# The two exponentials of the SSD chunk decays, moved behind the last logarithm of the GLA gates on ScalarE

## The chip, the core and the metric

The kernel runs on one core of a Trainium2 chip. The metric is the time of one execution on the device, in microseconds (us); lower is better. TensorE is called PE in the profile, VectorE DVE, ScalarE ACT, GpSimd POOL, and SyncE, which issues nearly all DMAs, SP. PEld is TensorE's load of the stationary operand.

## The reference

One layer of a hybrid encoder is applied to a prompt of 256 tokens and a sample of 512 tokens, each of width 1024. The input is normed and projected by one matrix (`w_in`), and three mixers share the result: a gated linear attention (GLA, 4 heads), a differential attention (4 heads) and a state space mixer (SSD, 8 heads). Their outputs go through `w_out`, and an MLP of width 4096 follows. GLA and SSD both run forwards and backwards over the tokens. Two pieces of it matter here:

```
# GLA: the gates
logg_f = jax.nn.log_sigmoid((r_f @ wg_f + bg_f)) / GLA_GATE_NORM

# SSD: steps, and the decay of the state over one chunk
dt_f = jax.nn.softplus(sdt[..., :SSD_HEADS] + dtb_f)
la = dt * a_neg
acum = jnp.cumsum(la, axis=1)
state = state * jnp.exp(acum[:, -1]) + ...
```

The last line's factor, the exponential of the sum of `la` over a whole chunk, is what the edit moves. The kernel computes it for six chunks of 128 tokens, two directions and eight heads.

## The kernel before, in words

All 768 tokens are worked on together as NT = 6 tiles of 128 tokens. Products with weights are split into high and low fp32r parts: a weight unit comes from DRAM in two halves (`wr`, two buffers), ScalarE casts the high part (`wh`, L134), VectorE subtracts to get the low part (`wl`, L135), and TensorE makes three matmuls per product (L98 to L100). `wh` and `wl` have two buffers each. `fm_unit` makes products with features on partitions (PSUM tiles `fm`, from the pool of three accumulators), `tm_unit` those with tokens on partitions (`tm`, the same pool). All other PSUM tiles (`tms`, `tmb`, `gate`, `kTp`, `U`, `att`) share the five buffers called `mx`.

The kernel is one straight program. A planner simulates all engines and fixes from it, before the kernel runs, the order of the instructions in each engine's queue; program order decides between instructions that are ready. On the chip each queue runs in order, with semaphores between the queues. `tc.high_priority()` lets instructions go ahead in that order. `tc.issue_after(ins)` keeps the instructions written inside it behind `ins` in the queue of that engine; it adds no semaphore.

Around the change the program is, in this order:

- `gla_v(0)`, then small loads and `glr_unit`, which gives the inputs of the GLA gates (`rst`) and of the SSD steps (`zdt`, 16 partitions).
- `ssd_dt()` (L503 to L564), called at L1034. Absolute value, exponential, logarithm and a correction give the softplus (L507 to L517). VectorE makes the running sums in each tile (`inc`, L522, called `dpre` in the profile) and the exclusive sums (`exc`, `dexc`, L523). SyncE writes both to DRAM (`scr`, L533 and L534), and the last column of `inc` to `scp` (L535). L538 reads `scp` back, broadcast to all partitions, as `ptb`. L543 takes two exponentials of it, one per half of the partitions, into `decs`. Then TensorE transposes the stacked rows (`tms`, L550; `tmb`, L555), ScalarE copies them out of PSUM (L552, L556), takes four exponentials of them (`ew`, L558 to L561), and VectorE multiplies two of those (L562, L563).
- `gla_gates(0)` and `gla_gates(1)` (L263 to L294), called at L1035. Each makes, for two directions, a gate product in two matmuls of 512 and 256 columns (L274), their absolute values and rectified values on ScalarE (L276, L277), one exponential (L278) and one logarithm (L279); VectorE adds and makes the running sums (L282 to L292). The list `log_ins` collects the four logarithms; the kernel's `tanh` (L196) uses its last entry with `issue_after`, since the tanh needs another function table in ScalarE.
- `gla_qk(0)`, `gla_core(pre[0], ...)` and so on (L1070 to L1077). The core's exponentials (L347 to L359) give `kst`, TensorE transposes it (`kTp`, L371), makes the states' products (`U`, L381), and then seven levels of differences (L428), exponentials (L432, L437), products (`eq`, L433, on VectorE; `ek`, L438, on GpSimd) and small matmuls (`att`, L412).

The planner interleaves these: matmuls of `gla_qk` fill TensorE while the gates run. The reader of `decs` is L660 in `ssd_states`, long after both GLA cores.

Of the kernel before, what the change touches and what calls it, by code (L numbers as in the profile page):

```python
# [13 lines left out]
AF = mybir.ActivationFunctionType  # L14
# [28 lines left out]
def hybrid_kernel(ctx, tc, io):  # L43
    nc = tc.nc
    mm, act, dve, pool = nc.tensor.matmul, nc.scalar, nc.vector, nc.gpsimd
# [10 lines left out]
    def nm(s):  # L56
        uid[0] += 1
        return f"{s}_{uid[0]}"
# [28 lines left out]
    def mx(name):  # L87
        return psm.tile([P, 512], F32, tag="mx", name=nm(name))
# [4 lines left out]
    def bc(ap, shape):  # L93
        return ap.to_broadcast(shape)
# [99 lines left out]
    log_ins = []  # L194
# [57 lines left out]
    def v128(t):  # L252
        return t.rearrange("p (c w) -> p c w", w=P)

    def prefix(dst, lg):

        dve.tensor_tensor_scan(dst, resetm[:dst.shape[0]], lg, 0.0, ALU.mult, ALU.add)
# [5 lines left out]
    def gla_gates(hp):  # L263


        c0 = hp * P
        pre = []
        for d, r in ((0, R_BF), (1, R_BB)):
            bias, nbias = col(r + hp), nbf[:, 2 * d + hp:2 * d + hp + 1]
            rngs = ((0, 512), (512, 256))  # L270
            zs = [mx("gate"), mx("gate")]
            t1, g = t3("gt1"), t3("gt2")
            for z, (o, n) in zip(zs, rngs):
                mm(z[:, :n], lhsT=wg[d][0:96, c0:c0 + P], rhs=rst[0:96, o:o + n], start=True, stop=True)  # L274
            for z, (o, n) in zip(zs, rngs):
                act.activation(t1[:, o:o + n], z[:, :n], AF.Abs, bias=bias)  # L276
                act.activation(g[:, o:o + n], z[:, :n], AF.Relu, bias=nbias, scale=-1.0)  # L277
            act.activation(t1, t1, AF.Exp, scale=-1.0)  # L278
            log_ins.append(act.activation(t1, t1, AF.Ln, bias=1.0).ins)  # L279
            pf = s3("pre")  # L280
            if d == 0:
                dve.tensor_tensor(g, g, t1, ALU.add)  # L282
                prefix(pf, g)
                pre.append(pf)
            else:
                tot = const.tile([P, NT, 1], F32, name=nm("tot"))
                dve.scalar_tensor_tensor(tot, v128(g)[:, :, 127:128], -1.0, v128(t1)[:, :, 127:128], op0=ALU.mult, op1=ALU.subtract)
                dve.scalar_tensor_tensor(v128(pf)[:, :, 1:128], v128(g)[:, :, 0:127], -1.0, v128(t1)[:, :, 0:127],
                                         op0=ALU.mult, op1=ALU.subtract)
                pool.memset(v128(pf)[:, :, 0:1], 0.0)  # L290
                prefix(pf, pf)
                dve.tensor_tensor(tot, tot, v128(pf)[:, :, 127:128], ALU.add)  # L292
                pre += [pf, tot]
        return pre  # L294
# [208 lines left out]
    def ssd_dt():  # L503

        ps_ = slice(96, 112)
        z, t1, u, l = zdt[ps_], t3("dz")[ps_], t3("dt2")[ps_], t3("dl")[ps_]
        act.activation(t1, z, AF.Abs)  # L507
        act.activation(t1, t1, AF.Exp, scale=-1.0)
        act.activation(l, t1, AF.Ln, bias=1.0)
        dve.tensor_scalar(u, t1, 1.0, -1.0, op0=ALU.add, op1=ALU.add)  # L510
        dve.tensor_tensor(t1, t1, u, ALU.subtract)
        act.activation(u, l, AF.Exp, scale=-1.0)
        dve.tensor_tensor(t1, t1, u, ALU.mult)
        dve.tensor_tensor(l, l, t1, ALU.add)
        stk = t3("stk")
        pool.memset(stk, 0.0)
        dve.scalar_tensor_tensor(stk[0:16], z, 0.0, l, op0=ALU.max, op1=ALU.add)  # L517
        dtl = t3("dtl")[ps_]

        dve.tensor_scalar(dtl, stk[0:16], sdtc[0:16, 3:4], -128.0, op0=ALU.mult, op1=ALU.max)  # L520
        inc, exc = t3("dpre")[ps_], t3("dexc")[ps_]
        dve.tensor_tensor_scan(inc, resetm[ps_], dtl, 0.0, ALU.mult, ALU.add)  # L522
        dve.tensor_tensor(exc, inc, dtl, ALU.subtract)  # L523
        act.copy(stk[32:48], inc)
        act.copy(stk[64:80], exc)
        tot = bc(v128(inc)[:, :, 127:128], [16, NT, P])
        dve.tensor_tensor(v128(stk[96:112]), tot, v128(inc), ALU.subtract)
        stb = t3("stb")
        dve.tensor_tensor(v128(stb[0:16]), tot, v128(exc), ALU.subtract)

        scr = dram.tile([16, T], F32, name="scr")
        scp = dram.tile([16, NT], F32, name="scp")
        nc.sync.dma_start(out=scr[0:8, :], in_=inc[0:8])  # L533
        nc.sync.dma_start(out=scr[8:16, :], in_=exc[8:16])  # L534
        nc.sync.dma_start(out=scp, in_=v128(inc)[:, :, 127])  # L535

        ptb = const.tile([P, 2, 8, NT], F32, name="ptb")
        nc.sync.dma_start(out=ptb.rearrange("p d h c -> p (d h c)"),  # L538
                            in_=bc(scp.rearrange("h c -> (h c)")[None, :], [P, 16 * NT]))
        decs = const.tile([P, NT, 2, 4], F32, name="decs")  # L540
        for g in range(2):
            gs = slice(64 * g, 64 * g + 64)
            act.activation(decs[gs], ptb[gs, :, 4 * g:4 * g + 4, :].rearrange("p d h c -> p c d h"), AF.Exp)  # L543

        tms = const.tile([P, NT, 40], F32, name="tms")
        tmb = const.tile([P, NT, 16], F32, name="tmb")
        for (a, b) in ((0, 4), (4, 6)):
            ps = mx("tms")
            for c in range(a, b):
                nc.tensor.transpose(ps[:, (c - a) * P:(c - a) * P + 112], stk[0:112, c * P:(c + 1) * P], ident[0:112, 0:112])  # L550
            for o, r, n in ((0, 0, 16), (16, 32, 8), (24, 72, 8), (32, 96, 8)):
                act.copy(tms[:, a:b, o:o + n], v128(ps)[:, :b - a, r:r + n])  # L552
        ps = mx("tmb")
        for c in range(NT):
            nc.tensor.transpose(ps[:, 16 * c:16 * c + 16], stb[0:16, c * P:(c + 1) * P], ident[0:16, 0:16])  # L555
        act.copy(tmb, ps[:, :96].rearrange("p (c r) -> p c r", c=NT))  # L556
        ew = const.tile([P, NT, 2, 2, 8], F32, name="ew")
        act.activation(ew[:, :, 0, 0, :], tms[:, :, 16:24], AF.Exp)  # L558
        act.activation(ew[:, :, 0, 1, :], tmb[:, :, 8:16], AF.Exp)
        act.activation(ew[:, :, 1, 0, :], tms[:, :, 32:40], AF.Exp)  # L560
        act.activation(ew[:, :, 1, 1, :], tms[:, :, 24:32], AF.Exp)  # L561
        dve.tensor_tensor(ew[:, :, 1, 0, :], ew[:, :, 1, 0, :], tms[:, :, 0:8], ALU.mult)  # L562
        dve.tensor_tensor(ew[:, :, 1, 1, :], ew[:, :, 1, 1, :], tms[:, :, 8:16], ALU.mult)  # L563
        return scr, decs, tms, ew  # L564

    def ssd_conv(us, xt, bcm):
        def conv(j):
# [417 lines left out]
    for i, nme in enumerate(("gla_wg_f", "gla_wg_b")):  # L985
# [4 lines left out]
        g = wgt[:, 256 * i:256 * i + 256]  # L990
# [30 lines left out]
    def col(r):  # L1021
        return cols[:, r:r + 1]
# [8 lines left out]
    qg8 = const.tile([P, 1], F32, name="qg8")  # L1031
    dve.tensor_scalar(qg8, col(R_QN), 0.125, None, op0=ALU.mult)

    dt = ssd_dt()  # L1034
    pre = [gla_gates(hp) for hp in range(2)]  # L1035

    masks = t2("masks").bitcast(U8)[:, :len(LOCAL) * 32].rearrange("p (l i) -> p l i", i=32)
    mraw = t2("mraw", n=len(LOCAL) * 32).rearrange("p (l i) -> p l i", i=32)
# [11 lines left out]
    for i in range(2):  # L1050
        g = qk16[:, i, None, :]
# [172 lines left out]
```

## Time and profile before

| | us |
|---|---|
| median of 3 runs | 1169.85 |
| lowest and highest | 1168.61, 1171.22 |
| the profiled execution | 1169.03 |
| its span, first to last instruction | 1167.2 |
| PE, DVE, ACT, POOL busy | 1110.8, 737.8, 563.9, 157.0 |

TensorE is busy in 95% of the span, at a mean granted clock of 0.976 of full speed. Matmuls are pipelined and their ends are modelled, so busy is not the same as at the peak. [...] The shares over the whole span tell little of a change in one place; the rows further down are read from the stretch around the edited lines, 60 to 110 us from the span's start, and from the first GLA core behind it.

### The profile page before, as it was taken

How to read it: one execution, taken by the hardware profiler on the slowest of the kernel's cores; microseconds unless marked ns; L12 is line 12 of the kernel's file. 1: busy time of each engine (PE TensorE's matmuls, PEld its weight loads, DVE VectorE, ACT ScalarE, POOL GpSimd, SP SyncE). 2: the span in 40 equal slices, each digit the busy share in tenths (PEclk: the TensorE clock that was granted, in tenths of full speed). 3: DMA queues.
4: the chain of work that ended last, by engine and by line, in shares of the span. 5: the costliest groups of instructions: out<-in, count | busy, mean ns of one | idle time of the engine just before them, and what ended most of it. 6: DMA issues, size and time to landing. Idle time of an engine off the chain costs nothing.

```text
span 1167.2 us, 19741 instructions
## 1 busy us (share of the span) xinstructions
PE 1110.8 (95%) x7868; PEld 978.6 (84%) x7868; DVE 737.8 (63%) x1298; ACT 563.9 (48%) x1119; POOL 157.0 (13%) x208
## 2 busy tenths in 40 slices
PE   7989797999998999899989999999999999999998
PEld 6989697999998986788877897788887787787786
DVE  6559859563697668887677786846544534434443
ACT  7476666554377237756666573425231332322321
POOL 1002425310401360110100012200000000000000
PEclk9989798899999999899999999999999999999999
DMA  6312021171534355445543549522323323233231
GB/s 196 85 40 74 4 64 38 41 240 39 162 96 127 111 160 167 126 144 177 195 144 120 187 145 305 200 92 73 108 72 108 101 80 108 77 104 99 82 109 72
DMA packets 118642, 136.41 MB, mean 117 GB/s; under 512 B 8936, under 2 KB 86790, under 8 KB 118550
## 3 DMA queue, kind: packets, MB, share of 16 engines
q1 hardware_dynamic: 118517, 135.14, 36.6%
q8 instruction: 62, 1.02, 0.3%
q14 instruction: 31, 0.25, 0.1%
q10 hardware_dynamic: 32, 0.01, 0.0%
HBM read 121.44 MB, written 13.68 MB: 116 GB/s over the span
## 4 chain that ended last, share of the span: by engine, by line
PE 61%; DVE 16%; DMA 11%; ACT 6%; issue 3%; POOL 2%; SPq 0%; DVEq 0%; ACTq 0%; POOLq 0%
PE tp L98 7%; DMA wr<-in_w_mlp 7%; PE tp L99 7%; PE tp L100 7%; PE fm L98 6%; PE fm L100 6%; PE fm L99 6%; PE tm L100 5%; PE tm L99 5%; PE tm L98 5%; DVE wl L135 4%; ACT wh L134 2%; DMA er<-scr 1%; DVE d L428 1%; DVE eq L433 1%
## 5 line engine op out<-in xcount | busy, mean ns | idle before, releaser
L134 ACT CAST wh<-wr 128x1024 fp32r<-128x1024 f32 x186 | 189.2, 1048 | 236.5 <-PE tp L100 129.2
L135 DVE TENSOR_TENSOR wl<-wr,wh 128x1024 fp32r<-128x1024 f32 x186 | 224.2, 1229 | 93.4 <-ACT wh L134 92.8
L100 PE MATMUL tm<-wh,hTl 128*128 128x256 f32 x576 | 168.7, 293 | 0.0
L98 PE MATMUL tm<-wh,hTh 128*128 128x256 f32 x576 | 166.8, 290 | 0.5 <-ACT xp L576 0.5
L99 PE MATMUL tm<-wl,hTh 128*128 128x256 f32 x576 | 166.8, 290 | 0.0
L901 DVE TENSOR_TENSOR xres<-tp,xres 128x512 f32<-128x512 f32 x116 | 77.8, 687 | 100.5 <-PE tp L100 100.3
L99 PEld LDWEIGHTS tm<-wl,hTh 128*128 128x128 f32 x576 | 112.4, 195 | 1.5 <-issue 1.0
L98 PEld LDWEIGHTS tm<-wh,hTh 128*128 128x128 f32 x576 | 112.2, 195 | 1.6 <-ACT xp L576 0.8
L100 PEld LDWEIGHTS tm<-wh,hTl 128*128 128x128 f32 x576 | 112.4, 195 | 0.7 <-issue 0.4
L99 PE MATMUL fm<-h2l,wh 128*128 128x512 f32 (+1 forms) x288 | 107.5, 374 | 0.0
L98 PE MATMUL fm<-h2h,wh 128*128 128x512 f32 (+1 forms) x288 | 107.1, 373 | 0.3 <-ACT h2h L185 0.3
L100 PE MATMUL fm<-h2h,wl 128*128 128x512 f32 (+1 forms) x288 | 107.0, 372 | 0.0
L98 PE MATMUL tp<-wh,uh 128*128 128x512 f32 x256 | 101.7, 397 | 0.6
L99 PE MATMUL tp<-wl,uh 128*128 128x512 f32 x256 | 101.0, 395 | 0.0
L100 PE MATMUL tp<-wh,ul 128*128 128x512 f32 x256 | 99.7, 395 | 0.0
L98 PE MATMUL fm<-h,wh 128*128 128x256 f32 x256 | 72.5, 284 | 3.4 <-ACT relu L947 3.4
L99 PE MATMUL fm<-h,wh 128*128 128x256 f32 x256 | 72.7, 285 | 0.0
L100 PE MATMUL fm<-h,wl 128*128 128x256 f32 x256 | 72.0, 284 | 0.6 <-DVE wl L135 0.6
L947 ACT ACTIVATE relu<-fm 128x256 f32<-128x256 f32 (+1 forms) x68 | 31.7, 469 | 73.2 <-PE fm L100 73.2
L98 PEld LDWEIGHTS fm<-h2h,wh 128*128 128x128 f32 x288 | 54.7, 191 | 10.7 <-ACT h2h L185 0.5
L100 PEld LDWEIGHTS fm<-h2h,wl 128*128 128x128 f32 x288 | 55.0, 191 | 10.1
L99 PEld LDWEIGHTS fm<-h2l,wh 128*128 128x128 f32 x288 | 54.9, 191 | 10.1
(325 smaller groups left out, 2446.7 us busy)
## 6 DMA issues: line engine op xcount, KB each, us to landing
wr<-in_w_mlp SPq DMA_DIRECT2D x128, 512.0 KB
wr<-in_w_in SPq DMA_DIRECT2D x30, 512.0 KB
wr<-in_w_out SPq DMA_DIRECT2D x24, 512.0 KB
ar<-scr SPq DMA_DIRECT2D x6, 512.0 KB
er<-scr SPq DMA_DIRECT2D x6, 512.0 KB
x<-in_x_sample SPq DMA_DIRECT2D x4, 512.0 KB
wr<-in_w_in SPq DMA_DIRECT2D x8, 256.0 KB
xres<-in_x_sample SPq DMA_DIRECT2D x4, 512.0 KB
```

Of the source, the lines that this page charges most:

```text
L98: mm(out, lhsT=lh, rhs=rh, start=first, stop=False)
L99: mm(out, lhsT=lh, rhs=rl, start=False, stop=False)
L100: mm(out, lhsT=ll, rhs=rh, start=False, stop=last)
L134: act.copy(hi, raw)
L135: dve.tensor_tensor(lo, raw, rd(hi), ALU.subtract)
L428: dve.tensor_tensor(D[i].rearrange("p b r i -> p b (r i)"), X.rearrange("p (b i) -> p b i", i=2 * s), bc(ref, [P, nb, 2 * s]), ALU.subtract)
L433: dve.tensor_tensor(parts(eq)[:, :, i], D[i][:, :, i], parts(q)[:, :, i], ALU.mult)
L901: dve.tensor_tensor(xres[t][:, cs], ps, xres[t][:, cs], ALU.add)
L947: act.activation(r, ps, AF.Relu)
```

## The change

`ssd_dt` becomes a generator with two steps. Its first step is all of it but the two exponentials. Then both gates are traced, and the second step traces the two exponentials, kept behind the last of the four logarithms in ScalarE's queue. The write of `scp`, the read of `ptb` and the reader of `decs` stay as they are.

```diff
         decs = const.tile([P, NT, 2, 4], F32, name="decs")
-        for g in range(2):
-            gs = slice(64 * g, 64 * g + 64)
-            act.activation(decs[gs], ptb[gs, :, 4 * g:4 * g + 4, :].rearrange("p d h c -> p c d h"), AF.Exp)
...
-        return scr, decs, tms, ew
+        yield
+
+        with tc.issue_after(log_ins[-1]):
+            for g in range(2):
+                gs = slice(64 * g, 64 * g + 64)
+                act.activation(decs[gs], ptb[gs, :, 4 * g:4 * g + 4, :].rearrange("p d h c -> p c d h"), AF.Exp)
+        yield scr, decs, tms, ew
...
-    dt = ssd_dt()
+    dt_steps = ssd_dt()
+    next(dt_steps)
     pre = [gla_gates(hp) for hp in range(2)]
+    dt = next(dt_steps)
```

## Rows read from the trace of the kernel before

**Rows 1.** Stretches: length; busy us of PE, PEld, DVE, ACT, POOL; clock; DMA.
```profile
63.00:86.00 23.00, 19.27 (x104) 18.46 (x103) 9.30 (x13) 15.73 (x43) 0.11 (x1) 0.85 0.15 49
86.00:105.00 19.00, 19.00 (x166) 19.00 (x164) 18.68 (x20) 13.99 (x25) 3.81 (x12) 1.00 0.19 56
105.00:143.00 38.00, 30.53 (x866) 28.64 (x864) 34.04 (x54) 23.37 (x56) 18.73 (x12) 0.85 0.11 31
```

**Rows 2.** Chain of waits in time order, 66 to 72 us: start, length, what.
```profile
66.51 4.25 DMA ptb<-scp
...
71.91 0.80 PE gate L274
```

**Rows 3.** ScalarE's timeline: start, length, instruction, idle time before and releaser.
```profile
63.11 0.48 ACT L313 ACTIVATE gk<-fm 128x384 f32<-128x384 f32 x1
70.78 0.58 ACT L543 ACTIVATE decs<-ptb 64x48 f32<-64x48 f32 x2 [7.20 <-DMA ptb<-scp]
71.38 0.80 ACT L552 COPY tms<-tms 128x64 f32<-128x64 f32 x8
...
74.03 0.47 ACT L276 ACTIVATE gt<-gate,cols 128x256 f32<-128x256 f32 x1
...
93.09 0.88 ACT L279 ACTIVATE gt<-gt 128x768 f32<-128x768 f32 x1
...
96.57 0.85 ACT L359 ACTIVATE kb<-pre 128x768 f32<-128x768 f32 x1 [1.34 <-DVE pre L288]
```

**Rows 4.** TensorE's timeline, 63 to 105 us.
```profile
63.45 0.74 PE L550 MATMUL tms<-ident,stk 112*128 112x112 f32 x6
...
64.59 0.62 PE L274 MATMUL gate<-rst,wg 96*128 96x512 f32 x2
65.05 0.34 PE L98 MATMUL fm<-hTh,wh 128*128 128x384 f32 x1
...
67.84 0.34 PE L99 MATMUL fm<-hTl,wh 128*128 128x384 f32 x1
71.91 0.80 PE L274 MATMUL gate<-rst,wg 96*128 96x512 f32 x1 [3.73 <-ACT tms L552]
...
104.36 0.82 PE L371 MATMUL kTp<-ident,kst 128*128 128x128 f32 x6
```

**Rows 5.** One stretch behind TensorE's idle time, columns as in rows 1.
```profile
74.00:76.00 2.00, 2.00 (x7) 2.00 (x7) 0.00 (x0) 2.00 (x6) 0.00 (x0) 0.50 0.00 0
```

**Rows 6.** Chain of waits: single matmuls, at half clock (first two) and full.
```profile
73.02 0.64 PE gate L274 x2
...
74.30 0.32 PE fm L100
...
77.44 0.23 PE gate L274
...
78.03 0.17 PE fm L100
...
79.94 0.12 PE gate L274
```

**Rows 7.** VectorE's timeline, 78 to 110 us.
```profile
78.62 0.96 DVE L282 TENSOR_TENSOR gt<-gt,gt 128x768 f32<-128x768 f32 x1 [5.53 <-ACT gt L279]
...
102.17 1.93 DVE L363 TENSOR_TENSOR kst<-gk,kf 64x768 f32<-64x768 f32 x2
...
109.64 0.34 DVE L388 SCALAR_TENSOR_TENSOR S<-S,dec,U 64x128 f32<-64x128 f32 x1 [2.17 <-ACT S L386]
```

**Rows 8.** Waits of SyncE's queue, 60 to 130 us: total, times, longest.
```profile
SPq L538 <- DMA scp<-dpre: 5.5, 1, 5.5
```

**Rows 9.** Waits of TensorE, 60 to 160 us: total, times, longest.
```profile
PE att L412 <- DVE eq L433: 3.4, 3, 1.6
```

**Rows 10.** Two stretches of the first GLA core, columns as in rows 1.
```profile
121.00:128.00 7.00, 6.03 (x118) 5.97 (x119) 5.95 (x6) 4.94 (x13) 6.05 (x5) 0.53 0.00 0
138.00:149.00 11.00, 9.08 (x221) 8.78 (x222) 7.25 (x14) 8.95 (x20) 0.00 (x0) 0.53 0.02 4
```

## The prediction, made before the changed kernel was run

> **What bounds the kernel now.** I began with the table of stretches, to see which engine is full where the edited lines run. Between 63 and 86 us no engine is: TensorE is busy 19.27 of 23 us at a mean granted clock of 0.85, ScalarE 15.73, VectorE 9.30. After that stretch the work is dense: TensorE is full from 86 to 105 us, and from 105 to 143 us, the first GLA core, VectorE has 34.04 of 38 us and TensorE 30.53 [rows 1]. So a stall at 63 to 86 us is not covered by a full engine; what remains to ask is who causes it.
>
> The chain of waits names it. After the prefix sums their last column goes to DRAM and comes back broadcast to all partitions (4.25 us for the way back alone), then come the two exponentials, and only then TensorE's next gate matmul [rows 2]. ScalarE's timeline shows why: its queue has L543 in front of the copies of `tms`. It stands 7.20 us on that DMA, runs L543 for 0.58 us, and then is busy without a gap of its own [rows 3]. TensorE's timeline shows the second victim: the transposes behind `tms` are done at 64.19 us, two gate matmuls follow, and after the matmul that starts at 67.84 us TensorE stands 3.73 us, because the next gate matmul needs one of the five `mx` buffers, which the `tms` copies free [rows 4]. [...] VectorE stands 5.53 us until the first logarithm hands it L282 at 78.62 us [rows 7].
>
> **The change part by part.**
>
> *L543 leaves its place.* ScalarE ends its copy of `gk` at 63.11 + 0.48 = 63.59 us. The `tms` copies are next and need the transposes, at 63.45 + 0.74 = 64.19 us. They start there in place of 71.38, so ScalarE gains 71.38 - 64.19 = 7.19 us at this point [rows 3, 4]. The whole stall with L543 is 7.78 us; the 0.6 between them is the wait for the transposes, which is late next.
>
> *The gates on ScalarE.* The sixth step behind the `tms` copies, L276 at 74.03 us, reads a 256-column gate product, and TensorE has 17 `fm` matmuls queued between the second gate matmul and the third, the first at 65.05 us and the last at 67.84. With the planner's order kept, TensorE comes to them at 67.84 + 0.34 = 68.18 us; a 512-column gate (0.23), an `fm` (0.17) and a 256-column gate (0.12) end at 68.70 us [rows 4, 6]. ScalarE, ready at 74.03 - 7.19 = 66.84, waits 1.86 us there, and is then 74.03 - 68.70 = 5.3 us earlier than before. VectorE's L282 hangs on this, so it comes about 5.3 us earlier too.
>
> *The stall on TensorE.* Its 3.73 us go: the buffer is free by about 65 us, before TensorE gets to it. The slow clock goes with them. From 71.91 to 77.44 us TensorE does one 512-column gate, one pair of a 256 and a 512, one single 256 and 13 `fm` matmuls in 5.53 us. [...] Together TensorE gains 3.73 + 2.6 = 6.3 us. The five buffers do not cut this: the seventh gate, at 77.44 us, takes a buffer that ScalarE frees about 1 us after L276 at 74.03; that is now 69.7, and TensorE comes to it at 77.44 - 6.3 = 71.1 us.
>
> *L543 at its new place.* The same two instructions, 0.58 us, stand behind the last logarithm, which ran at 93.09 us and would run near 87.8. Their input has been in SBUF since 70.8 us, so they wait for nothing. Behind them on ScalarE is the exponential of `eb`; its queue has an idle gap of 1.34 us before L359 shortly after, which takes the 0.58 [rows 3]. Cost zero; without that gap it is 0.58. The reader of `decs`, L660, comes behind both GLA cores, in the state sums of the SSD part.
>
> *DMAs.* None is added, removed or moved. SyncE still stands 5.5 us on the write of `scp` before it can issue the read of `ptb`, with weight loads behind it [rows 8]. Those loads are for a unit that TensorE reaches only near the kT transposes at 104 us, so this wait stays and stays hidden.
>
> *How the gain passes on.* TensorE is full from 77 to 105 us, so its 6.3 us arrive at the kT transposes. VectorE, 5.3 us earlier, must have the first kst product by then; before, it ended at 102.17 + 0.95 = 103.1 us (half of the pair of L363) against the transposes' start at 104.36 [rows 4, 7], and 97.8 against 98.1 just fits. From there VectorE waited for TensorE, 2.17 us through ScalarE's copy of S [rows 7], so VectorE being one us behind is taken up in that wait. Behind it the work keeps its order and moves as a whole.
>
> Sum: between 5.3 (ScalarE's and VectorE's gain) and 6.3 (TensorE's); I take 6.0, nearer to TensorE's, since at 109.64 us it is VectorE that waits. The ends for the range are 3.73 (the idle time alone, the clock lost anyhow) and 7.78 (ScalarE's whole stall, if the planner also puts the gate matmuls earlier). The profiled execution took 1169.03 us, a span of 1167.2 with 1.8 around it; 1169.03 - 6.0 = 1163.0. It lies 0.8 under the median of the runs, 1169.85, against which the number is given: 1163.8.
>
> **The clock.** The traces show it at half in more places than the one that goes: 0.53 on average from 121 to 128 us and again from 138 to 149 us, both following stretches in which TensorE waited for VectorE or GpSimd [rows 10]. [...]
>
> **The rivals.**
>
> *A dip comes back.* The 2.6 us of slow matmuls are won at 72 to 77 us and given back in a longer dip at 121 to 149 us. For it: two dips already lie there [rows 10]. Against it: VectorE, not TensorE, is fuller there [rows 1], so slow matmuls are partly hidden. Gain 6.0 - 2.6 = 3.4: 1166.4 us.
>
> *Hidden in the first core.* The stretch from 105 to 143 us is bound by VectorE [rows 1]; if the planner lets TensorE's or GpSimd's part slip there, or VectorE's chain starts late because ScalarE takes the two exponentials and a weight split before `eb`, most of the gain goes: 0 to 2 us are left, 1168 to 1170. Against it: VectorE starts 5.3 us earlier by the same step.
>
> *The planner sorts the first core worse: slower.* The order of every queue comes out of the planner's own clock, and removing 0.58 us on ScalarE at 64 us and adding it at 88 can turn close decisions in the stretch from 105 to 143 us. The place is the wait of the `att` matmuls for VectorE's `eq`, 3.4 us in three waits [rows 9]; if it doubles, TensorE idles 3.4 us more, and if this brings another half-clock dip as long as that from 138 to 149 us, back-to-back matmuls lose 11 x 0.47 = 5.2 us. Together 8.6 against the 6.0 won: 2.6 slower, 1172.5 us. It decides from where idle and dip exceed 6.0. Against it: no row shows a wait that doubles after so small a move; but none excludes it.
>
> *The edit does not act.* Another instruction that waits for a late DMA moves to the front of ScalarE's queue; nothing is won, 1169.9. Of the steps traced next to L543 no other has input from DRAM, so this is improbable.
>
> **How the numbers follow.** About 0.2%, 2.3 us, is what a measurement of this kernel can tell from no change. Forecast (gain of 4.5 to 7.8): 0.63, its own range 1162.0 to 1165.4. Dip comes back: 0.12, still faster by more than 2.3. Hidden in the first core: 0.11, of which 0.01 ends just beyond 2.3. Slower: 0.11. Edit does not act: 0.03. So faster 0.76, same 0.13, slower 0.11. The range reaches from 1160.0 (the 7.78, and a later dip that gets shorter by as much as 2 us) to 1169.6, which takes in the returning dip and most of the hidden case.
>
> **What would show it.** Right: no 7 us of idle time before L543; the `tms` copies at about 64.2 us; TensorE without idle time from 63 to 105 us and its granted clock at 1.00 there; L282 near 73 us; L543 behind the fourth L279, at about 88 us, with no wait; the kT transposes near 98 us. Wrong: the stall is gone and the kT transposes are not earlier (something else held them), or they are 6 us earlier and the end of the first core, then 143 us, is not (hidden there, or a dip).

## The result, and the profile after

Fifteen executions of each kernel give a median of 1163.22 us (1161.09 to 1169.06) after the change and 1170.59 us (1167.65 to 1173.41) before; the ratio is 0.9946, with a 95% interval of 0.9934 to 0.9958. By this ratio the change takes off 6.3 us (5 to 7.7); the two medians lie 7.4 us apart, inside that interval. The forecast was 1163.8 us.

As far as the traces show, every engine runs the same instructions in the same order as before; the two exponentials alone have moved. So the two traces can be laid side by side. The table of stretches of the changed kernel, with the columns of [rows 1]:

```profile
63.00:86.00 23.00, 23.00 (x159) 22.60 (x158) 16.09 (x19) 22.09 (x52) 0.34 (x2) 1.00 0.14 49
86.00:105.00 19.00, 19.00 (x166) 19.00 (x165) 15.70 (x19) 10.63 (x22) 5.79 (x14) 1.00 0.38 111
105.00:143.00 38.00, 29.29 (x847) 27.39 (x846) 32.48 (x53) 25.75 (x62) 16.56 (x11) 0.87 0.01 3
```

TensorE, busy 19.27 of 23 us from 63 to 86 us before, is now full at a granted clock of 1.00. ScalarE's timeline of the changed kernel shows the place that was left and the new one:

```profile
62.44 0.48 ACT L313 ACTIVATE gk<-fm 128x384 f32<-128x384 f32 x1
63.63 0.80 ACT L549 COPY tms<-tms 128x64 f32<-128x64 f32 x8 [0.71 <-PE tms L547]
...
66.50 0.46 ACT L276 ACTIVATE gt<-gate,cols 128x256 f32<-128x256 f32 x1
...
85.56 0.88 ACT L279 ACTIVATE gt<-gt 128x768 f32<-128x768 f32 x1
86.29 0.60 ACT L566 ACTIVATE decs<-ptb 64x48 f32<-64x48 f32 x2
...
89.05 0.85 ACT L359 ACTIVATE kb<-pre 128x768 f32<-128x768 f32 x1 [0.75 <-DVE pre L288]
```

Where 7.20 us of waiting stood [rows 3], 0.71 us for the transposes are left; the exponentials run at 86.29 us without a wait, and the gap in front of L359 has shrunk from 1.34 to 0.75 us, by the 0.6 us that they take. TensorE's timeline, to compare with [rows 4]:

```profile
63.05 0.74 PE L547 MATMUL tms<-ident,stk 112*128 112x112 f32 x6
...
67.44 0.34 PE L99 MATMUL fm<-hTl,wh 128*128 128x384 f32 x1
67.61 0.40 PE L274 MATMUL gate<-rst,wg 96*128 96x512 f32 x1
...
70.61 0.40 PE L274 MATMUL gate<-rst,wg 96*128 96x512 f32 x1
...
97.70 0.82 PE L371 MATMUL kTp<-ident,kst 128*128 128x128 f32 x6
```

The third gate follows its predecessor at once. The row at 70.61 us is the seventh gate, which stood here before:

```profile
77.28 0.40 PE L274 MATMUL gate<-rst,wg 96*128 96x512 f32 x1
```

From the `tms` transposes to the kT transposes TensorE took 104.36 - 63.45 = 40.91 us before and takes 97.70 - 63.05 = 34.65 us now: 6.26 us less. I measure from the `tms` transposes, since their own start differs from one execution to the next (63.05 to 64.86 us in the runs here), and the rest moves with them. VectorE, as in [rows 7]:

```profile
64.86 0.21 DVE L560 TENSOR_TENSOR ew<-ew,tms 128x48 f32<-128x48 f32 x1 [0.87 <-ACT ew L558]
...
71.09 0.96 DVE L282 TENSOR_TENSOR gt<-gt,gt 128x768 f32<-128x768 f32 x1 [5.90 <-ACT gt L279]
...
94.64 1.93 DVE L363 TENSOR_TENSOR kst<-gk,kf 64x768 f32<-64x768 f32 x2
...
102.98 0.34 DVE L388 SCALAR_TENSOR_TENSOR S<-S,dec,U 64x128 f32<-64x128 f32 x1 [3.03 <-ACT S L386]
```

The first of these instructions is where VectorE lost its time before:

```profile
72.75 0.21 DVE L563 TENSOR_TENSOR ew<-ew,tms 128x48 f32<-128x48 f32 x1 [8.10 <-ACT ew L561]
```

The profiled execution itself took 1169.06 us, the slowest of the fifteen, with a span of 1167.3 us: as long as the one before the change, although it is 6.7 us ahead at the kT transposes. The reader of `decs` marks where that went. The first row is of the kernel before, the other three are of the changed kernel in this execution and in two more (e1 and e7 below); the columns are durations and first and last start:

```profile
L660 DVE TENSOR_TENSOR st<-st,decs x4: 415/420/427, 460.5 to 467.1; 128x256 f32<-128x256 f32 x4
```
```profile
L663 DVE TENSOR_TENSOR st<-st,decs x4: 416/421/426, 452.2 to 458.9; 128x256 f32<-128x256 f32 x4
```
```profile
L663 DVE TENSOR_TENSOR st<-st,decs x4: 414/420/426, 452.7 to 459.4; 128x256 f32<-128x256 f32 x4
```
```profile
L663 DVE TENSOR_TENSOR st<-st,decs x4: 409/421/426, 452.8 to 459.5; 128x256 f32<-128x256 f32 x4
```

From there to the end of the span it is 1167.3 - 452.2 = 715.1 us here, 706.9 and 708.3 us in the two others (spans 1159.6 and 1161.1). The kernel before took 706.7 us from its same instruction in the execution shown (460.5, span 1167.2), and 708.5 in a second one (461.8, span 1170.3). So a single execution can lose 8 us in the later part, where weights are awaited, and one profile alone would have hidden the gain. Up to this reader, measured from the `tms` transposes, the changed kernel leads by 7.3 to 8.8 us in these executions, about 1 us more than at the kT transposes; no run shows where that 1 us comes from. The medians, and the part up to the kT transposes, are what can be compared.

### The profile page after: what moved, and what is told of

It is laid out like the page before. It is cut to its first block, busy times and chain, and to the rows that moved or that the text cites. A ratio compares the mean times of both kernels' runs of the same rounds, so it can differ in the third digit from the quotient of the medians.

```text
span 1167.3 us, 19741 instructions
## 1 busy us (share of the span) xinstructions
PE 1109.1 (95%) x7868; PEld 974.9 (84%) x7868; DVE 738.5 (63%) x1298; ACT 563.6 (48%) x1119; POOL 158.0 (14%) x208
## 4 chain that ended last, share of the span: by engine, by line
PE 64%; DVE 15%; DMA 10%; ACT 5%; issue 3%; POOL 2%; SPq 0%; DVEq 0%; ACTq 0%; POOLq 0%
PE tp L98 8%; DMA wr<-in_w_mlp 7%; PE fm L98 7%; PE tp L99 7%; PE fm L100 7%; PE fm L99 7%; PE tp L100 7%; PE tm L99 5%; PE tm L100 5%; PE tm L98 5%; DVE wl L135 4%; ACT wh L134 2%; DMA er<-scr 2%; DVE d L428 1%; DVE eq L433 1%
## 5 line engine op out<-in xcount | busy, mean ns | idle before, releaser
L98 PE MATMUL fm<-h,wh 128*128 128x256 f32 x256 | 73.2, 287 | 4.0 <-ACT relu L950 4.0
```

The lines of the kernel that those rows point to most:

```text
L98: mm(out, lhsT=lh, rhs=rh, start=first, stop=False)
```

## The experiments

Each ratio below is to the kernel before on the same chip.

**The changed kernel, again (e1, e7).** No edit.

> The changed kernel itself, a second time. Theory (the wait): the gain is made between 63 and 105 us, so TensorE again has no idle time there, the kT transposes start near 98 us (98.1 forecast, 97.7 in the first profile of the changed kernel), and the ratio is again near 0.995. In the first profile of the changed kernel the whole gain was lost between 500 and 750 us, to longer waits for weights and for er. If that is chance from one execution to the next, this profile differs there and its span is near 1161; if it belongs to the change, the span is again near 1167.

> The changed kernel a third time, for one more profile of the stretch from 500 to 750 us. If the loss there in the first profile was chance of one execution, the kT transposes come near 98 us again and the lead over the kernel before, some 7 to 8 us at 480 us, is mostly kept to the end; if it comes back, it belongs to the change.

e1: median 1164.19 us, ratio 0.9943 (0.9923 to 0.9962), span 1159.6; e7: one execution, 1162.86 us. In both, 34.65 us lie between the two groups of transposes (63.88 to 98.53, and 63.10 to 97.75): the same to 0.01 us as in the first profile. The loss of the first profile did not come back.

**The kernel before, again (e8).** No edit.

> The kernel before, once more, for the spread of the same stretch without the change. If longer waits for weights come and go from one execution to the next, the stretch from 480 to 760 us differs between the two profiles of this kernel by some us too, with the order of all instructions the same; if it agrees within 1 us, the loss of the changed kernel's first profile there is harder to put down to chance. The kT transposes come near 104.4 us, TensorE idles 3.7 us in front of the third gate.

The transposes stand at 64.12 and 105.71 us, 41.59 apart; TensorE idled 4.1 us and ScalarE stood 7.9 us on the trip through DRAM, both longer than in the first profile. Against this execution the change gains 6.9 us up to the kT transposes, against the first profile 6.3. The waits of ScalarE from 480 to 760 us for the MLP's weights differ between the executions of either kernel. The rows are total, times and longest, for the kernel before in its first and second execution, then the changed kernel in its first and in e1:

```profile
ACT wh L134 <- DMA wr<-in_w_mlp: 50.3, 32, 4.6
```
```profile
ACT wh L134 <- DMA wr<-in_w_mlp: 54.5, 31, 5.7
```
```profile
ACT wh L134 <- DMA wr<-in_w_mlp: 56.8, 32, 6.0
```
```profile
ACT wh L134 <- DMA wr<-in_w_mlp: 50.4, 30, 4.1
```

50 to 57 us, without a pattern by kernel: the profile puts this spread down to the landing of weights, not to the change. The executions with the longer waits also have the longer rest of the span behind the reader of `decs`, but the waits grow by 6.5 us and the rest by 8.4, so not all of it is accounted for. Why the weights land later in some executions stays open.

**In place, without DRAM (e2).**

```diff
-            act.activation(decs[gs], ptb[gs, :, 4 * g:4 * g + 4, :].rearrange("p d h c -> p c d h"), AF.Exp)
+            act.activation(decs[gs], ident[gs, 48 * g:48 * g + 48].rearrange("p (d h c) -> p c d h", d=2, h=4), AF.Exp)
```

(held behind the last copy into `stk`, so that they stay ahead of the copies of `tms`; they now run in front of two casts of `wh` and the copy of `gk` too, which is three instructions further forward than before the change)

> The two exponentials stay in front of the copies of tms, as before the change, but read a constant that lies in SBUF in place of ptb; the trip through DRAM still runs. What it leaves out: the decays are not the reference's. All other instructions keep their order. Theory (the wait): taking the wait away without moving anything is worth as much as the move, kT transposes at 98 +- 0.5 us, ratio 0.995. Rival (the place: the 0.58 us of the exponentials, or their position in ScalarE's queue, is what counts): kT transposes stay near 104 us, ratio 1.000.

Median 1163.89 us, ratio 0.9932 (0.9912 to 0.9952). ScalarE's and TensorE's timelines of this kernel:

```profile
62.60 0.59 ACT L544 ACTIVATE decs<-ident 64x48 f32<-64x48 f32 x2
```
```profile
64.86 0.74 PE L551 MATMUL tms<-ident,stk 112*128 112x112 f32 x6
...
99.50 0.82 PE L371 MATMUL kTp<-ident,kst 128*128 128x128 f32 x6
```

99.50 - 64.86 = 34.64 us. The absolute start of the kT transposes, 99.5, lies 1 us outside the 98 +- 0.5 that was expected: the `tms` transposes already began 1.8 us later here than in the first profile of the changed kernel. The distance between the two is the same as with the change, and the ratio is that of the theory. In front of the `tms` copies the exponentials cost nothing once their input does not come through DRAM. It is the wait, not the place or the 0.6 us.

**Written later, but not held (e9).**

```diff
-        with tc.issue_after(log_ins[-1]):
+        with ExitStack():
```

> The two exponentials are written behind the gates, as in the change, but without being held behind the last logarithm. The planner then puts them into ScalarE's queue where they were before the change, in front of the copies of tms: it takes their input to be there by then. Theory (only the place in the queue counts): as before the change, a wait of 7 to 8 us in front of them, kT transposes near 104.4 to 105.7 us, ratio 1.000. Rival (writing them later frees the queue by itself): kT transposes near 98 us, ratio 0.995.

Ratio 1.0009 (0.9988 to 1.0030). ScalarE's timeline shows the wait back in its old place:

```profile
71.95 0.58 ACT L566 ACTIVATE decs<-ptb 64x48 f32<-64x48 f32 x2 [8.21 <-DMA ptb<-scp]
```

The transposes are 105.51 - 63.69 = 41.82 us apart. So `issue_after` is the part of the change that acts; the later place in the source alone does nothing. That the planner counted the input as landed by then is my reading of the order it made; no run shows its reckoning.

**Behind `ew` (e3): the buffers come free, ScalarE still waits.**

```diff
...
+        with tc.issue_after(ew_last):
+            for g in range(2):
+                gs = slice(64 * g, 64 * g + 64)
+                act.activation(decs[gs], ptb[gs, :, 4 * g:4 * g + 4, :].rearrange("p d h c -> p c d h"), AF.Exp)
         dve.tensor_tensor(ew[:, :, 1, 0, :], ew[:, :, 1, 0, :], tms[:, :, 0:8], ALU.mult)
```

(the exponentials are taken out of their old place; `ew_last` is the last of the four `ew` exponentials in the source)

> The two exponentials stand behind the copies of tms and two of the exponentials of ew, in front of the gates' steps: the buffers come free at about 65 us, but ScalarE still stands on the trip through DRAM, until about 70 us. Theory (two victims: TensorE through the buffers, ScalarE and VectorE through the gates' steps): TensorE's third gate is not late (68 us), its sixth gate waits for ScalarE's reads for about 1.5 us, the first logarithm comes near 75.9 us, and the kT transposes, now held by VectorE's kst, come near 101 us: half of the gain. Rival A (the buffers are all of it): kT near 98 us. Rival B (ScalarE's queue is all of it): the kT transposes gain no more than the first logarithm, 1.8 us, 102.5.

Median 1173.86 us, ratio 1.0025 (1.0009 to 1.0040): slower than before. TensorE's timeline, then the stretch at half clock in this kernel and the same in the kernel before, with the columns of [rows 1]:

```profile
68.29 0.40 PE L274 MATMUL gate<-rst,wg 96*128 96x512 f32 x1
...
73.61 0.58 PE L274 MATMUL gate<-rst,wg 96*128 96x256 f32 x1 [2.47 <-ACT gt L277]
...
104.46 0.82 PE L371 MATMUL kTp<-ident,kst 128*128 128x128 f32 x6
```
```profile
73.20:79.90 6.70, 6.29 (x20) 6.19 (x21) 1.82 (x2) 6.70 (x14) 0.11 (x1) 0.50 0.04 14
```
```profile
70.20:77.00 6.80, 5.09 (x16) 4.90 (x17) 0.34 (x2) 6.17 (x24) 0.00 (x0) 0.50 0.40 140
```

The third gate is on time at 68.29 us, as expected, and the sixth waits for ScalarE: 2.47 us where 1.5 was expected. But I expected half of the gain, and 104.46 - 63.73 = 40.73 us is 0.2 less than in the first profile of the kernel before (0.9 less than in e8). The miss is the clock: it fell to 0.50 after this shorter idle time too, for as long as before, and less of it fell into idle time: TensorE worked 6.29 us at half clock in place of 5.09, and about half of that is loss, since a matmul of 384 columns takes 0.32 us there in place of 0.17 [rows 6]. The planner also put four more `tm` matmuls, 0.12 us each, in front of the kT transposes (166 in place of 162). So 1.26 us of idle time are won, 0.6 us are lost to the clock and 0.46 to these matmuls: 0.2 us are left, as measured. By the gain to the kT transposes rival B, no more than the first logarithm gains, is the nearest; but since clock and order came in between, this run does not tell the two victims apart. Behind the kT transposes, too, the planner sorted the work in another way; those of the second core show what came of it (first and last start in the last columns):

```profile
L371 PE MATMUL kTp<-ident,kst x24: 272/273/274, 104.5 to 186.8; 128*128 128x128 f32 x24
```

82.3 us lie between the two cores, where the kernel before has 76.1 (104.4 to 180.5). The medians differ by only 3.0 us; the profiled execution, 1178.11 us, was the slowest of its twelve, and no run shows where the rest went.

**Behind the first and behind the third logarithm (e4, e10).**

```diff
-        with tc.issue_after(log_ins[-1]):
+        with tc.issue_after(log_ins[0]):
```

> The two exponentials stand behind the first of the four logarithms in place of the last, at about 71 us, when their input has just landed. Theory (the wait): any place behind the landing is as good, no wait in front of them, kT transposes at 98 +- 0.7 us, ratio within 0.002 of the change's. Rival (it has to be behind the last logarithm, since 0.58 us in front of the later gates delays VectorE's chain): kT transposes 0.6 us or more later than with the change. The planner also changes some order behind 105 us here, so that the stretch to 105 us decides.

> The two exponentials stand behind the third logarithm, some 7 us before the last. Their input has landed, so they wait for nothing; the kT transposes come near 98 us, as with the change. Behind 110 us the planner orders some instructions of ScalarE, VectorE, TensorE and SyncE in another way than with the change. Theory (the wait is all, the rest is the planner's order): the gain to the kT transposes is 6.3 us again, and the total lies between the change's and that of the place behind the first logarithm, ratio 0.995 to 0.9965. Rival (0.58 us among the gates costs by itself): the kT transposes are already 0.6 us later than with the change.

e4 has a ratio of 0.9964 (0.9952 to 0.9976), e10 (with `log_ins[2]`) 0.9957 (0.9935 to 0.9979). Neither waits in front of the exponentials. The transposes are 98.58 - 63.58 = 35.00 us apart in e4 and 98.13 - 63.24 = 34.89 in e10, so 0.35 and 0.24 us more than with the change: less than the rival's 0.6. Even this is not the price of the exponentials. The rows show TensorE's `tm` matmuls between the two transposes in the changed kernel, e10 and e4 (length, busy time, clock, DMA):

```profile
63.04:97.69 34.65, 18.90 (x162) 1.00 0.20 63
```
```profile
63.23:98.12 34.89, 19.13 (x164) 1.00 0.19 63
```
```profile
63.57:98.57 35.00, 19.24 (x165) 1.00 0.20 63
```

The planner put two and three more of them in front of the kT transposes, and they take 0.23 and 0.34 us: the whole difference. Behind that, too, the two differ from the change in the planner's order. The kT row for e4:

```profile
L371 PE MATMUL kTp<-ident,kst x24: 271/273/273, 98.6 to 176.8; 128*128 128x128 f32 x24
```

78.2 us between the cores, 2 us more than before; e10 has 76.1 (98.1 to 174.2), and the interval of its ratio holds the change's. Each of the three places behind the landing keeps the gain up to the first core, but for the matmuls that the planner moved in front of it; the 2 us that e4 loses behind it go with the other order there, and no run takes that order apart.

**TensorE kept busy during the wait (e5).**

```diff
+            if hp == 0 and d == 0:
+                for _ in range(60):
+                    mm(zs[1][:, 256:512], lhsT=wg[d][0:96, c0:c0 + P], rhs=rst[0:96, 0:256], start=True, stop=True)
```

> The kernel before, with 60 extra matmuls of 256 columns behind the second gate matmul (into unused columns of its PSUM buffer; nothing reads them), about 7.0 us of work at full clock, so that TensorE has no idle time while ScalarE stands on the trip through DRAM. The wait itself stays. The 17 fm matmuls that ran there before come behind it. Theory (the half clock follows from TensorE's idle time and cost 2.6 us): the granted clock is 1.00 from 63 to 86 us, and the kT transposes come at 104.4 + 2.95 (17 x 0.17 displaced) - 2.6 = 104.7 +- 0.7 us. Rival (the half clock comes from something else there, such as the weights landing at 70 to 74 us): the clock falls to 0.50 all the same and the kT transposes come at 107 us or later.

The one execution took 1175.01 us; the kT transposes came at 107.88 us. The extra work did not cover all: the trip through DRAM ended 1 us later, and TensorE still had two short waits. Nor is the start of the kT transposes the number that was meant, since the planner left only 151 `tm` matmuls in front of them in place of 162. TensorE's timeline of the two waits, and a stretch behind them:

```profile
72.93 0.96 PE L274 MATMUL gate<-rst,wg 96*128 96x512 f32 x3 [0.68 <-ACT tms L555]
75.07 0.39 PE L274 MATMUL gate<-rst,wg 96*128 96x256 f32 x1 [1.19 <-ACT gt L280]
```
```profile
76.00:80.00 4.00, 4.00 (x16) 4.00 (x16) 0.00 (x0) 4.00 (x8) 0.00 (x0) 0.57 0.02 4
```

Both numbers of the theory missed, and the kT transposes at 107.9 us fit the rival's "107 or later". By itself this run decides nothing: the clock fell, but TensorE had idled. The rival falls by the changed kernel: there the weights land at the same time with TensorE busy, and the clock stays at 1.00. The stretch in the changed kernel (the last columns are clock, DMA share and GB/s):

```profile
70.00:72.00 2.00, 2.00 (x13) 1.95 (x12) 0.91 (x1) 2.00 (x4) 0.00 (x0) 1.00 1.07 380
```

The twelve profiles agree: in the seven in which TensorE does not wait from 63 to 86 us its granted clock there is 1.00, in the five in which it waits (both of the kernel before, e3, e5, e9) it is 0.85 to 0.93.

**The trip doubled, at the new place (e6).**

```diff
-        nc.sync.dma_start(out=ptb.rearrange("p d h c -> p (d h c)"),
-                            in_=bc(scp.rearrange("h c -> (h c)")[None, :], [P, 16 * NT]))
+        scq = dram.tile([16, NT], F32, name="scq")
+        nc.gpsimd.dma_start(out=scq, in_=scp)
+        nc.gpsimd.dma_start(out=ptb.rearrange("p d h c -> p (d h c)"),
+                            in_=bc(scq.rearrange("h c -> (h c)")[None, :], [P, 16 * NT]))
```

> The changed kernel with the trip through DRAM doubled: the last column is copied once more from DRAM to DRAM, and that copy and the broadcast read are issued by GpSimd in place of SyncE. All compute engines keep their order. Theory (at the new place the trip is covered, the input landing near 70 us and being needed near 86): the longer trip, landing near 77 to 82 us, costs nothing; no wait in front of the exponentials, kT transposes at 98 +- 0.5 us, ratio near 0.995. Rival (the cover is thin): ScalarE waits in front of the exponentials and the kT transposes come later by the same.

Ratio 0.9952 (0.9932 to 0.9971). The trace of this kernel, the DMA issues and ScalarE's step:

```profile
L539 POOL DMA_DIRECT2D scq<-scp x1: 717/717/717, 66.6 to 66.6; - x1
L540 POOL DMA_DIRECT2D ptb<-scq x1: 577/577/577, 71.2 to 71.2; - x1
```
```profile
87.52 0.60 ACT L568 ACTIVATE decs<-ptb 64x48 f32<-64x48 f32 x2
```

The read is issued at 71.2 us in place of 65 to 67, lands some 3 us later, and the exponentials at 87.52 us wait for nothing. The transposes are 34.65 us apart again. Thirteen microseconds of cover are left even then. The doubled trip landed near 74 us, not at the 77 to 82 expected, so it tried the cover less than was meant.

## Why the prediction was right, step by step

*The cause* held. e2 takes the wait away and leaves the exponentials in front of the `tms` copies, and gains the same 6.3 us to 0.01; e9 moves the lines without moving the place in the queue and gains nothing.

*TensorE's term*, 3.73 us of idle time and 2.6 of slow matmuls, was forecast at 6.3 and measured at 6.26 against the execution from which it was worked out; against e8, which idled 4.1 us, it is 6.94. So the match to 0.04 us holds for that one execution. The idle time and the half clock went together: the changed kernel has no idle time from 63 to 105 us and a granted clock of 1.00 there. The 2.6 us are my estimate from the lengths in [rows 6], by which the matmuls from the third gate to the seventh need 13 x 0.17 + 2 x 0.23 + 2 x 0.12 = 2.9 of the 5.53 us between 71.91 and 77.44 us; no run shows this term by itself, since none removed the half clock without the idle time (e5 was to, and did not). What the two traces show in its place is 2.4: the same matmuls took 77.28 - 71.91 = 5.37 us before and take 70.61 - 67.61 = 3.00 us now. So 2.4 us of the 6.3 are the clock and 3.9 the wait; the terms of the sum were 2.6 and 3.73.

*ScalarE's term* was wrong. The prediction has ScalarE wait 1.86 us at what it calls the sixth step behind the `tms` copies (the eighth in the timeline), L276 at 74.03 us, for a gate matmul behind the 17 `fm`. That step reads the second matmul of the first pair, a 256-column one, done at 65 us; my row shows the pair under the form of its first. In the changed kernel the step runs at 66.50 us without a wait. VectorE's L282 then gained not 5.3 us but 7.1, measured from the `tms` transposes: 78.62 - 63.45 = 15.17 before, 71.09 - 63.05 = 8.04 now, close to the 7.19 worked out for the step ahead of it. It did not change the sum, because TensorE's 6.3 is the smaller of the two and ends last at the kT transposes; VectorE's surplus of 0.9 us shows as a wait at L388 that grew from 2.17 to 3.03 us. The 6.0 that I took, between a wrong 5.3 and a right 6.3, should have been 6.3. The wait that the prediction names for VectorE was the wrong one, too: the 5.53 us before L282 are still there, at 5.90; what went is the wait before the product of `ew`, from 8.10 us (L563) to 0.87 (L560).

*The new place* cost nothing, by the gap that was named for it (1.34 us, now 0.75). e6 shows that the cover has 13 us to spare.

*Passing on.* Behind the kT transposes the gain was to move as a whole. From the first core's transposes to the second's it is 76.1 and 76.4 us before (first profile and e8) and 75.7, 76.3 and 76.0 us with the change (first profile, e1, e7). No two of these differ by more than 0.7 us. So nothing was hidden in the first core, and the forecast's dip that comes back did not come: the granted clock over this stretch is 0.89 in both executions before and 0.93, 0.89 and 0.89 in the three with the change. The traces show one of three executions of the changed kernel with less half clock (0.93), and a time between the cores that is 0.3 to 0.7 us shorter there.

*The slower rival*, a worse order by the planner, is real but was not met. The change left every other instruction in its place. e3 and e4 did not, and were 6 and 2 us longer between the two cores; e3 came out slower than the kernel before.

*The total.* A ratio of 0.9946 is 6.3 us, TensorE's term, but its interval is 5 to 7.7 us, so the agreement to a tenth is luck. The median lies 0.6 us from the forecast and inside its own range, and part of this is luck as well: the forecast set out from 1169.85 us and a gain of 6.0, while in the measurement the kernel before stood at 1170.59 and the medians lie 7.4 apart.

## What to carry to other kernels

Here an instruction that waited 7.20 us for a trip through DRAM [rows 3] cost 6.3 us through what was queued behind it on its engine, not its own 0.6 us; look for what it blocks (here copies that free PSUM buffers for TensorE), then put it behind work that does not need it, far enough that the landing is past (here at 86.29 us, with the landing at 70.8 before the change). Moving the line in the source can do nothing where a planner orders the queues (e9, ratio 1.0009): check the order that comes out, and that the rest of it has stayed. And judge a change of half a per cent by medians and by the stretch it touches: here a single execution of each kernel showed the same span.

## What the runs showed that I had not expected

The half clock came with shorter idle times too: with 2.47 us (e3) the granted clock was 0.50 from 73.2 to 79.9 us, about as long as with the 3.73 us before the change (70.2 to 77.0 us), and with two waits of 0.68 and 1.19 us (e5) it was still 0.57 from 76 to 80 us. It did not come with every one: with a wait of 1.03 us at 131.4 us in the kernel before, the granted clock was 1.00 from 129 to 138 us. So shortening the stall of TensorE by 1.26 us (e3) brought the kT transposes only 0.2 us nearer, and only removing it returned the 2.4 us. The other surprise is how exactly a stretch repeats: 34.64 or 34.65 us in five executions of three kernels (the changed one, e2 and e6), against 8 us of spread in the rest of the span.
